# A conformer/SSD block on one core: first pieces' lower halves by adding loads, earlier sums for two units, other banks for the first units, y scaled on ScalarE

## Chip, core and metric

One core of a Trainium2 chip. The metric is the device time of one execution of the program in microseconds (us); less is better. The engines go by these names: PE is TensorE (matmuls), DVE is VectorE, ACT is ScalarE, POOL is GpSimd, and SP issues the loads of weights.

## What is computed

The reference is one block with two branches and a feed forward, all in float32, for 512 tokens of 1024 features:

```python
h = rms_norm(x, mix_pre_g)
proj = h @ w_in
conv_out = conformer_conv_branch(...)     # gated, 31-tap depthwise conv, layer norm, silu, matmul
ssm_out = ssd_branch(...)                 # 4-tap conv, chunked state space scan, then:
#   y = y * silu(z); per group of 256 channels: y * rsqrt(mean(y * y) + eps); y @ out_w
mixed = (g_conv * conv_out + g_ssm * ssm_out) @ w_out
x = x + rms_norm(mixed, mix_post_g)
h = rms_norm(x, ffn_pre_g)
gt, up = jnp.split(h @ w_gate_up, 2, axis=-1)
x = x + rms_norm((silu(gt) * up) @ w_down, ffn_post_g)
```

## The kernel before

Matmuls keep float32 precision by splitting: each operand is cast to a rounded upper half (`hi`), and a lower half (`lo`) is what the cast left over; `mm3` (L165) multiplies hi by hi, hi by lo and lo by hi. So each piece of weights, 128 x 1024, needs a load (`w_raw`, SP, a ring of 5 raw tiles), a cast on ACT and a lower half. In the mixer the lower half has two ways (`w_part`, L131): a subtraction on DVE (L139), or, for every second piece, a negated copy of hi on ACT (L136) and a load from DRAM that adds the raw weights to it, issued by POOL (L137).

The mixer works group by group over 8 groups. `s3` (L588) ends with the norm of y: four squares on ACT (L621), the factor on POOL (`power`), and four multiplications by it on DVE (L624). The transposes of y on PE come in `s4`, one group later.

The output projection (`tm_wo`) runs over four tiles of 128 tokens (t) and eight pieces (k), in the order of `steps`. After a tile's last step `residual(t)` makes the norm, the residual and a diagonal matrix `dg` of the next norm's factors: DVE (L937, L943, L947), ACT (L814) and POOL (L822) take turns. `transposed(t)` multiplies the tile by `dg` (PE, `ptr`, L960), reads the result as `xg`, and makes hi and lo of the moving operands b11, b21, and for odd tiles t1, t2, then in `rest` b22, t3, t4.

The feed forward's gate and up products run over 22 units of 256 columns (u). Each uses a recursion with seven products instead of eight (`product`, 12 matmuls each): `first(u)` (a11 by b11, a12 by b21, into X and Y of a bank), `second(u)` (s2 by t2, s1 by t1, s3 by t3), `third(u)` (s4 by b22, a22 by t4). `second` begins by copying X (ACT, L1075) and adding Y (DVE, L1067), since its s2 product goes on in X. The weights of a unit are two raw pieces. `prep_a` makes hi and lo of the first (a11, a12). `prep_s` makes four sums on DVE (L898 to L903), in the raw tiles, and hi and lo of them: three halves (s2/s4, s1, s3/a22). All go through `halve` (cast on ACT, L877; subtraction on DVE, L878). The tiles for them come in turn from two pools, eight pairs in all (`pair_of_tiles`), so a unit can be prepared when the unit some two and a half before it has been multiplied. Units 0 and 1 have their first pieces prepared at (t, k) = (2, 1). The order within an engine's queue is drawn up by the framework's scheduler from dependencies and program order; `not_before` adds an order without a wait, and `hold` holds those in force.

PSUM has 8 banks; from the output projection on, `bank` (L798) hands them out in turn: `tm_wo` 0 to 7, the transposes of tiles 0 to 2 banks 0 to 5, xy0 and xy1 banks 6 and 7, and so on.

Of the kernel before, what the change touches and what calls it, by code (L numbers as in the profile page):

```python
# [10 lines left out]
F32 = mybir.dt.float32  # L11
# [63 lines left out]
EARLY_U = 4  # L75
DMA_EVERY = 2
DMA_FROM = 8
MOV_AT = 192

TAPS_GLU = 12  # L80
# [29 lines left out]
def block_kernel(ctx: ExitStack, tc: tile.TileContext, x, xT, prm, hp, gp, w, out):  # L110
# [477 lines left out]
    def s3(g):  # L588
        s = st[g]
        hs = slice(HG * g, HG * (g + 1))  # L590
        y = s["y"]
        for n in range(2):
            dve.tensor_tensor(out=y[:, 2 * n : 2 * n + 2], in0=s["yd"][n], in1=y[:, 2 * n : 2 * n + 2], op=ALU.add)
        pa, pb = aux_tile(f"pYa{g}"), aux_tile(f"pYb{g}")
        pY = [None, pa[:, :GW], pa[:, GW:], pb[:, :GW]]
        for c in range(1, NT):
            pe.matmul(
                pY[c], s["C"][:, c * P : (c + 1) * P], s["prev"][:, c - 1].rearrange("p h d -> p (h d)"),
                start=True, stop=True,
            )  # L600
        yo = ssd.tile([P, NT - 1, HG, HD], F32, tag="yo", name=f"yo{g}")
        dve.tensor_tensor(
            out=yo[:, 0:2], in0=pa.rearrange("p (c h d) -> p c h d", c=2, h=HG),
            in1=b3(eacs[:, 1:3, hs], HD), op=ALU.mult,
        )
        dve.tensor_tensor(
            out=yo[:, 2], in0=pb[:, :GW].rearrange("p (h d) -> p h d", h=HG),
            in1=b3(eacs[:, 3, hs], HD), op=ALU.mult,
        )
        dve.tensor_tensor(out=y[:, 1:], in0=y[:, 1:], in1=yo, op=ALU.add)  # L610
        yz = y.rearrange("p c h d -> p c (h d)")
        if "zb" in s:
            for n, zb in enumerate(s["zb"]):
                dve.tensor_tensor(out=yz[:, 2 * n : 2 * n + 2], in0=yz[:, 2 * n : 2 * n + 2], in1=zb, op=ALU.mult)
        else:
            dve.tensor_tensor(out=yz, in0=yz, in1=s["z"], op=ALU.mult)
        ss = ssd.tile([P, NT], F32, tag="ss", bufs=2, name=f"ss{g}")
        rs = ssd.tile([P, NT], F32, tag="rs", bufs=2, name=f"rs{g}")
        for c in range(NT):
            jk = ssd.tile([P, GW], F32, tag="jk", name="jk")  # L620
            act.activation(jk, yz[:, c, :], AF.Square, accum_out=ss[:, c : c + 1])  # L621
        power(rs, ss, 1.0 / GW, RMS_EPS, NT)
        for c in range(NT):
            dve.tensor_scalar(out=yz[:, c, :], in0=yz[:, c, :], scalar1=rs[:, c : c + 1], scalar2=None, op0=ALU.mult)  # L624

    ys = {}

# [167 lines left out]
    dr2 = ctx.enter_context(tc.tile_pool(name="dr2", bufs=1, space=DRAM))  # L795
    x2d = dr2.tile([T, D], F32, name="x2d")

    def bank(name):  # L798
        return in_turn("big", 0, 8, name)

    def tm_tiles(key):
        return [[bank(f"tm_{key}_{t}_{n}") for n in range(2)] for t in range(NT)]
# [69 lines left out]
            w_raw(r)  # L872
        return raws[n]

    def halve(names, u, src, room):
        hi, lo = room
        a_ = act.copy(hi, src)  # L877
        d_ = dve.tensor_tensor(out=lo, in0=src, in1=hi.bitcast(F32), op=ALU.subtract)  # L878
        if hold:
            not_before(a_, hold[0])  # L880
            not_before(d_, hold[1])
        for i, n in enumerate(names):
            c = slice(i * T, (i + 1) * T)
            forms[u, n] = hi[:, c], lo[:, c]

    def prep_a(u, room=None):

        if u < NF and (u, "a11") not in forms:
            halve(("a11", "a12"), u, g_raw(u, 0), room or pair_of_tiles())

    def prep_s(u):

        if u >= NF or (u, "s1") in forms:
            return
        ra, rb_ = g_raw(u, 0), g_raw(u, 1)
        (a11, a12), (a21, a22) = [(r[:, :T], r[:, T:]) for r in (ra, rb_)]
        s1_ = w2.tile([P, T], F32, tag="s1", bufs=2, name=f"s1_{u}")
        sum_ = dve.tensor_tensor(out=s1_, in0=a21, in1=a22, op=ALU.add)  # L898
        if hold:
            not_before(sum_, hold[1])  # L900
        dve.tensor_tensor(out=a21, in0=a11, in1=a21, op=ALU.add)
        dve.tensor_tensor(out=a11, in0=s1_, in1=a11, op=ALU.add)
        dve.tensor_tensor(out=a12, in0=a11, in1=a12, op=ALU.add)  # L903
        halve(("s2", "s4"), u, ra, pair_of_tiles())
        halve(("s1",), u, s1_, [w2.tile([P, T], F32R, tag=tg, bufs=2, name=f"{tg}_{u}") for tg in ("dhi", "dlo")])
        room = pair_of_tiles()

        def last():
            halve(("s3", "a22"), u, rb_, room)

        if u:
            last()
        return last

    def product(ps, u, wn, mn, start):

# [34 lines left out]
    def transposed(t):  # L951
# [2 lines left out]
        xr, dg = xrs[t]  # L954
        xg = []
        for n in range(2):
            pt = bank(f"ptr{t}_{n}").rearrange("p (k q) -> p k q", k=KB)
            for k in range(KB):
                c = slice((KB * n + k) * P, (KB * n + k + 1) * P)
                m = pe.matmul(pt[:, k, :], xr[:, c], dg, start=True, stop=True)  # L960
# [13 lines left out]
        def halved(name, src, sign=1.0):  # L974
# [12 lines left out]
            mark["hi"], mark["lo"] = h_, l_  # L987

        if t % 2 == 0:
            halved("b11", xg[0])  # L990
# [5 lines left out]
        dve.tensor_tensor(out=t1, in0=b11, in1=xg[0], op=ALU.subtract)  # L996
        dve.tensor_tensor(out=t2, in0=t1, in1=xg[1], op=ALU.add)
        halved("t1", t1)
        halved("t2", t2, -1.0)

        def rest():
            halved("b22", xg[1])
# [2 lines left out]
            dve.tensor_tensor(out=t2, in0=t2, in1=b21, op=ALU.subtract)  # L1005
            halved("t4", t2)

        return rest
# [6 lines left out]
    for t, k in steps:  # L1015
# [9 lines left out]
            for u in range(2):  # L1025
                prep_a(u, [m[:, u] for m in first_room])
        if (t, k) == (2, 5):
            others = transposed(1)
        if (t, k) == (3, 5):
            with tc.issue_after(mark["pe"].ins):  # L1030
                transposed(2)

    X, Y, V = {}, {}, {}

    def first(u):

        xy = bank(f"xy{u}")
        X[u], Y[u] = xy[:, :HB], xy[:, HB:]
        product(X[u], u, "a11", "b11", True)
        product(Y[u], u, "a12", "b21", False)  # L1040

    prep_a(2)
    prep_a(3)
    last_s = prep_s(0)
    mark["chain"] = True
    for u in range(3):
        first(u)
    rest = transposed(3)
    pb.close()
    h2e = h2.enter_context(tc.tile_pool(name="h2e", bufs=2))  # L1050
    hold[:] = [mark["hi"], mark["lo"]]
    last_s()
    rest()
    first(3)
    mark["chain"] = False
    prep_s(1)
    hold.clear()
# [5 lines left out]
    sg = {}  # L1063
    c1, c2 = slice(0, HB), slice(HB, T)

    def add(to, ps):
        dve.tensor_tensor(out=to, in0=ps, in1=to, op=ALU.add)  # L1067

    def second(u):
        f, e = u // 2, u % 2  # L1070
        if e == 0:
            dst = sg[f] = [h2e.tile([P, T], F32, tag=f"sg{i}", bufs=2, name=f"sg{f}_{i}") for i in range(2)]
        else:
            dst = [f32[:, 2 * f + i, :] for i in range(2)]
        act.copy(dst[0][:, c1], X[u])  # L1075
        add(dst[0][:, c1], Y[u])
# [173 lines left out]
```

## Time and profile before

| | us |
|---|---|
| median of 3 runs | 1067.81 (1066.97 to 1069.09) |
| profiled execution | 1069.47 |
| its span, first to last instruction | 1067.7 |
| PE busy | 1049.2 (98%) |
| DVE busy | 782.5 (73%) |
| ACT busy | 594.7 (56%) |
| POOL busy | 79.7 (7%) |

A busy share says how long an engine had an instruction in it, not that the instruction ran without a stall. Matmuls overlap, so the distance from one start to the next is what a matmul costs; it is less than its duration. In a timeline a bracket at the end of a line gives the idle time of the engine before the instruction and what ended it. The mixer lasts to about 666 us, the output projection to 714.7, the units of the feed forward to 941.7, the down projection to the end.

### The profile page before, as it was taken

The page shows a single profiled execution, that of the slowest core. Times are in us where ns is not written, and L with a number is a line of the kernel's source. Part 1 is how long each engine was busy: PE and PEld are TensorE (multiplying, and loading weights), DVE is VectorE, ACT ScalarE, POOL GpSimd, SP SyncE. Part 2 cuts the span into 40 slices and gives each one's busy share as a digit, 9 for nine tenths or more (in the row PEclk, how much of TensorE's full clock was granted, in tenths as well). Part 3 has the DMA queues.
Part 4 walks back from the last instruction along what each step waited for, and adds up shares of the span by engine and source line. Part 5 has one row for each costly group of instructions (what it writes and reads, how often), then busy time and mean ns, then how long its engine had stood idle before and what let it go on. Part 6 is the DMA issues. An engine that isn't in the chain of part 4 may idle for free.

```text
span 1067.7 us, 15144 instructions
## 1 busy us (share of the span) xinstructions
PE 1049.2 (98%) x5897; PEld 912.1 (85%) x5897; DVE 782.5 (73%) x1150; ACT 594.7 (56%) x978; POOL 79.7 (7%) x104
## 2 busy tenths in 40 slices
PE   8999999999999999999999999998999999999997
PEld 7988889888888888888888888888999999988886
DVE  7899995977695979497876365569998788643334
ACT  7767749684859375934322672456564554532222
POOL 0002001110111011101100000010000000000000
PEclk9999999999999999999999999999999999999999
DMA  8476653566436553654442232422433243353302
GB/s 294 132 186 209 157 139 89 151 168 165 101 119 159 157 123 116 161 122 111 116 122 82 76 99 79 178 85 93 146 134 118 84 135 100 119 197 99 99 1 79
DMA packets 38088, 136.10 MB, mean 127 GB/s; under 512 B 4480, under 2 KB 4992, under 8 KB 36992
## 3 DMA queue, kind: packets, MB, share of 16 engines
q1 hardware_dynamic: 28368, 97.31, 27.7%
q0 software_dynamic: 6912, 29.36, 13.8%
q10 hardware_dynamic: 2736, 8.46, 2.2%
q8 instruction: 46, 0.75, 0.3%
q14 instruction: 26, 0.21, 0.1%
HBM read 130.85 MB, written 4.26 MB: 127 GB/s over the span
## 4 chain that ended last, share of the span: by engine, by line
PE 79%; DVE 11%; ACT 4%; issue 3%; DMA 1%; POOL 1%; SPq 0%; DVEq 0%; POOLq 0%; ACTq 0%
PE tm_wd L169 4%; PE tm_wd L167 4%; PE tm_wd L168 4%; PE xy L167 3%; PE xy L169 3%; PE xy L168 3%; PE px L169 2%; PE px L168 2%; PE px L167 2%; PE yd L585 2%; PE pz L168 2%; PE pz L169 2%; PE pso L168 2%; PE pz L167 2%; PE pso L169 2%
## 5 line engine op out<-in xcount | busy, mean ns | idle before, releaser
L133 ACT CAST whi<-raw 128x1024 fp32r<-128x1024 f32 (+2 forms) x135 | 137.6, 1029 | 186.6 <-PE pso L168 40.0
L407 DVE SCALAR_TENSOR_TENSOR a<-v,prm_t,a 128x511 f32<-128x511 f32 (+16 forms) x240 | 179.6, 752 | 10.0 <-ACT a L404 7.0
L139 DVE TENSOR_TENSOR wlo<-raw,whi 128x1024 fp32r<-128x1024 f32 (+3 forms) x95 | 112.5, 1187 | 39.5 <-ACT whi L133 39.5
L167 PE MATMUL tm_wd<-whi,fh 128*128 128x512 f32 x160 | 62.2, 389 | 0.0
L168 PE MATMUL tm_wd<-wlo,fh 128*128 128x512 f32 x160 | 62.2, 389 | 0.0
L169 PE MATMUL tm_wd<-whi,fl 128*128 128x512 f32 x160 | 62.2, 389 | 0.0
L137 POOL DMA_DIRECT2D wlo<-in_w x40 | 35.6, 890 | 329.5 <-ACT wlo L136 162.0
L168 PE MATMUL pz<-wlo,hhi 128*128 128x512 f32 (+2 forms) x160 | 56.3, 352 | 0.2
L169 PE MATMUL pz<-whi,hlo 128*128 128x512 f32 (+2 forms) x160 | 55.8, 351 | 0.0
L167 PE MATMUL pz<-whi,hhi 128*128 128x512 f32 (+2 forms) x160 | 55.5, 353 | 0.0
L877 ACT CAST whi_g<-raw 128x1024 fp32r<-128x1024 f32 x40 | 41.1, 1052 | 23.9 <-DVE raw L903 13.0
L878 DVE TENSOR_TENSOR wlo_g<-raw,whi_g 128x1024 fp32r<-128x1024 f32 x40 | 48.0, 1220 | 8.6 <-ACT whi_g L877 8.6
L1120 DVE TENSOR_TENSOR fl<-f,fh 128x512 fp32r<-128x512 f32 x20 | 13.8, 691 | 50.4 <-ACT fh L1119 50.4
L168 PE MATMUL pso<-yl,whi 128*128 128x512 f32 x128 | 49.9, 390 | 0.4 <-DVE yl L639 0.4
L167 PE MATMUL px<-hhi,whi 128*128 128x512 f32 x128 | 50.2, 392 | 0.0
L169 PE MATMUL pso<-yh,wlo 128*128 128x512 f32 x128 | 49.9, 390 | 0.0
L167 PE MATMUL pso<-yh,whi 128*128 128x512 f32 x128 | 49.9, 392 | 0.0
L169 PE MATMUL px<-hhi,wlo 128*128 128x512 f32 x128 | 49.8, 389 | 0.0
L168 PE MATMUL px<-hlo,whi 128*128 128x512 f32 x128 | 49.8, 389 | 0.0
L1119 ACT CAST fh<-f 128x512 fp32r<-128x512 f32 x20 | 12.4, 620 | 60.4 <-PE tm_wd L168 60.4
L390 ACT ACTIVATE L<-L,nacs 128x128 f32<-128x128 f32 x128 | 40.9, 391 | 5.7 <-POOL L L384 5.5
L136 ACT ACTIVATE wlo<-whi 128x1024 fp32r<-128x1024 f32 x40 | 42.3, 1056 | 0.2
(422 smaller groups left out, 3207.8 us busy)
## 6 DMA issues: line engine op xcount, KB each, us to landing
raw<-in_w SPq DMA_DIRECT2D x177, 512.0 KB, 3.6
wlo<-in_w POOLq DMA_DIRECT2D x40, 512.0 KB, 5.6
L<-scr POOLq DMA_DIRECT2D x8, 1024.0 KB, 6.3
xT<-in_xT SPq DMA_DIRECT2D x8, 256.0 KB, 5.4
xr<-in_x ACTq DMA_DIRECT2D x4, 512.0 KB, 4.3
x2d<-xr ACTq DMA_DIRECT2D x4, 512.0 KB, 2.6
x<-x2d ACTq DMA_DIRECT2D x1, 2048.0 KB, 10.3
gpost<-in_gp ACTq DMA_DIRECT2D x2, 512.0 KB, 8.0
```

The lines of the kernel that those rows point to most:

```text
L133: act.copy(hi[:, c], src[:, c])
L136: act.activation(lo[:, c], hi[:, c].bitcast(F32), AF.Copy, scale=-1.0)
L137: pool.dma_start(lo[:, c], w[n][:, c].bitcast(F32R), accum_op=ALU.add)
L139: dve.tensor_tensor(out=lo[:, c], in0=src[:, c], in1=hi[:, c].bitcast(F32), op=ALU.subtract)
L167: mark["pe"] = pe.matmul(ps, lh, rh, start=start, stop=False, skip_group_check=more)
L168: pe.matmul(ps, lh, rl, start=False, stop=False, skip_group_check=more)
L169: mark["pe3"] = pe.matmul(ps, ll, rh, start=False, stop=stop, skip_group_check=more)
L390: act.activation(L[:, h, c, :], L[:, h, c, :], AF.Exp, bias=nacs[:, c, HG * g + h : HG * g + h + 1])
L407: return dve.scalar_tensor_tensor(out=va[j][:, d:], in0=vs[j][:, : T - d], scalar=col("dw_w", j * KC + KC - 1 - d), in1=va[j][:, d:], op0= ...
L585: pe.matmul(yd[c // 2][:, c % 2, h, :], s["L"][:, h, c, :], s["xdt"][:, c, h, :], start=True, stop=True)
L877: a_ = act.copy(hi, src)
L878: d_ = dve.tensor_tensor(out=lo, in0=src, in1=hi.bitcast(F32), op=ALU.subtract)
```

## The change

- `halve` takes an argument `again`. With it, the lower half is not subtracted on DVE: ACT writes the negated hi, and POOL issues a load that adds the raw weights to it, as in the mixer. `prep_a` uses it from unit 2 on (`ADD_FROM`).
- `prep_a(2)` and `prep_a(3)` move from behind the output projection to its steps (3, 1) and (3, 2); the sums of unit 0 (`prep_s(0)`) move to step (3, 4). `prep_s` returns its three halves as a function for units 0 and 1: unit 0's are made before the first products, unit 1's after t1 to t4; unit 1's sums come after `first(0)`.
- `transposed` returns t1 and t2 as a function `sums` of its own, ahead of `rest`. `begin(u)`, the copy of X and the addition of Y, is taken out of `second`; unit 0's comes before `sums` of tile 3. `first(3)` now stands behind unit 1's halves.
- The transposes of tiles 0, 2 and 3 use banks 0 and 1, those of tile 1 banks 2 and 3; xy0 to xy3 use banks 2 to 5; the turn goes on at bank 6.
- In `s3` the four multiplications of y by its factor go from DVE to ACT.

```diff
-            dve.tensor_scalar(out=yz[:, c, :], in0=yz[:, c, :], scalar1=rs[:, c : c + 1], scalar2=None, op0=ALU.mult)
+            act.activation(yz[:, c, :], yz[:, c, :], AF.Copy, scale=rs[:, c : c + 1])
...
-    def bank(name):
-        return in_turn("big", 0, 8, name)
+    def bank(name, n=None):
+        return in_turn("big", 0, 8, name) if n is None else yd_tile(n, name)
...
-    def halve(names, u, src, room):
+    def halve(names, u, src, room, again=None):
+
         hi, lo = room
         a_ = act.copy(hi, src)
-        d_ = dve.tensor_tensor(out=lo, in0=src, in1=hi.bitcast(F32), op=ALU.subtract)
+        if again is not None:
+            d_ = act.activation(lo, hi.bitcast(F32), AF.Copy, scale=-1.0)
+            pool.dma_start(lo, again.bitcast(F32R), accum_op=ALU.add)
+        else:
+            d_ = dve.tensor_tensor(out=lo, in0=src, in1=hi.bitcast(F32), op=ALU.subtract)
...
-            halve(("a11", "a12"), u, g_raw(u, 0), room or pair_of_tiles())
+            again = w[seq[("gu", 2 * u)]] if u >= ADD_FROM else None
+            halve(("a11", "a12"), u, g_raw(u, 0), room or pair_of_tiles(), again)
...
-        halve(("s2", "s4"), u, ra, pair_of_tiles())
-        halve(("s1",), u, s1_, [w2.tile([P, T], F32R, tag=tg, bufs=2, name=f"{tg}_{u}") for tg in ("dhi", "dlo")])
-        room = pair_of_tiles()
-
-        def last():
-            halve(("s3", "a22"), u, rb_, room)
-
-        if u:
-            last()
-        return last
+
+        def halves():
+            halve(("s2", "s4"), u, ra, pair_of_tiles())
+            halve(("s1",), u, s1_, [w2.tile([P, T], F32R, tag=tg, bufs=2, name=f"{tg}_{u}") for tg in ("dhi", "dlo")])
+            halve(("s3", "a22"), u, rb_, pair_of_tiles())
+
+        if u > 1:
+            halves()
+        return halves
...
-            pt = bank(f"ptr{t}_{n}").rearrange("p (k q) -> p k q", k=KB)
+            pt = bank(f"ptr{t}_{n}", 2 * (t == 1) + n).rearrange("p (k q) -> p k q", k=KB)
...
+        if (t, k) in ((3, 1), (3, 2)):
+            prep_a(k + 1)
+        if (t, k) == (3, 4):
+            halves = prep_s(0)
...
-        xy = bank(f"xy{u}")
+        xy = bank(f"xy{u}", 2 + u if u < EARLY_U else None)
...
-    prep_a(2)
-    prep_a(3)
-    last_s = prep_s(0)
+    halves()
     mark["chain"] = True
     for u in range(3):
         first(u)
-    rest = transposed(3)
+        if u == 0:
+            halves = prep_s(1)
+    sums, rest = transposed(3)
     pb.close()
     h2e = h2.enter_context(tc.tile_pool(name="h2e", bufs=2))
-    hold[:] = [mark["hi"], mark["lo"]]
-    last_s()
+    begin(0)
+    sums()
     rest()
+    hold[:] = mark["t3"]
+    halves()
+    hold[:] = mark["t4"]
     first(3)
     mark["chain"] = False
-    prep_s(1)
+    turn["big"] = 1 + EARLY_U
+    prep_s(2)
```

## Rows read from the trace of the kernel before

**Rows 1.** The page's first part: busy us, share of the span, instructions.
```profile
PE 1049.2 (98%) x5897; PEld 912.1 (85%) x5897; DVE 782.5 (73%) x1150; ACT 594.7 (56%) x978; POOL 79.7 (7%) x104
```
**Rows 2.** Stretches: length, busy us (instructions) by engine, granted clock, DMA share, GB/s.
```profile
225.00:680.00 455.00, 452.80 (x2203) 378.45 (x2202) 331.23 (x477) 257.63 (x418) 42.70 (x53) 1.00 0.47 129
714.70:745.50 30.80, 26.51 (x204) 25.42 (x204) 28.05 (x45) 20.00 (x40) 1.72 (x2) 0.94 0.24 75
745.50:768.50 23.00, 23.00 (x204) 23.00 (x204) 22.63 (x35) 12.64 (x21) 0.00 (x0) 1.00 0.45 153
768.50:830.00 61.50, 60.55 (x519) 59.20 (x518) 57.22 (x87) 34.36 (x57) 0.00 (x0) 1.00 0.38 121
830.00:900.00 70.00, 67.95 (x578) 66.79 (x577) 58.27 (x87) 36.68 (x61) 0.00 (x0) 1.00 0.33 106
900.00:941.70 41.70, 41.70 (x370) 41.70 (x369) 26.97 (x44) 19.18 (x34) 0.00 (x0) 1.00 0.32 102
```
**Rows 3.** TensorE's waits, whole span, longest entry: us in total, times, longest.
```profile
PE xy L167 <- DVE sg L1067: 2.8, 4, 1.3
```
**Rows 4.** Timeline of TensorE, 715 to 743: start, us, line, operation [idle before].
```profile
715.74 0.38 PE L167 MATMUL xy<-b11h,a01h 128*128 128x256 f32 x1 [0.88 <-DVE mg L937]
...
724.32 1.95 PE L960 MATMUL ptr<-dg,xr 128*128 128x128 f32 x16
...
729.92 0.35 PE L167 MATMUL xy<-t2h,whi_g 128*128 128x256 f32 x1 [0.79 <-DVE sg L1067]
...
741.97 0.54 PE L169 MATMUL xy<-t2h,clo_g 128*128 128x256 f32 x1 [1.17 <-DVE clo_g L878]
742.30 0.41 PE L167 MATMUL xy<-t2h,chi_g 128*128 128x256 f32 x1
```
**Rows 5.** Timeline of VectorE, 723 to 727.
```profile
723.49 0.29 DVE L947 TENSOR_SCALAR dg<-ident,rs_b 128x128 f32<-128x128 f32 x1 [0.44 <-POOL rs_b L822]
...
725.49 1.22 DVE L878 TENSOR_TENSOR wlo_g<-raw,whi_g 128x1024 fp32r<-128x1024 f32 x1 [0.51 <-ACT whi_g L877]
726.63 0.68 DVE L967 TENSOR_TENSOR xg<-ptr,prm_t 128x512 f32<-128x512 f32 x1
```
**Rows 6.** Timeline of TensorE, two of its later waits.
```profile
845.85 0.39 PE L167 MATMUL xy<-t2h,chi_g 128*128 128x256 f32 x1 [1.31 <-DVE sg L1067]
...
866.69 0.38 PE L167 MATMUL xy<-t2h,whi_g 128*128 128x256 f32 x1 [0.35 <-DVE sg L1067]
```
**Rows 7.** Timeline of VectorE ahead of these two waits.
```profile
844.77 0.69 DVE L898 TENSOR_TENSOR s<-raw 128x512 f32<-128x512 f32 x1 [1.18 <-DMA raw<-in_w]
845.38 0.42 DVE L1067 TENSOR_TENSOR sg<-xy,sg 128x256 f32<-128x256 f32 x1
...
864.75 1.22 DVE L878 TENSOR_TENSOR wlo_g<-raw,whi_g 128x1024 fp32r<-128x1024 f32 x1
...
866.22 0.41 DVE L1067 TENSOR_TENSOR sg<-xy,sg 128x256 f32<-128x256 f32 x1
```
**Rows 8.** Instructions on tile wlo, 100 to 600: duration ns min/median/max, first and last start.
```profile
L136 ACT ACTIVATE wlo<-whi x34: 1040/1051/1086, 105.6 to 539.2; 128x1024 fp32r<-128x1024 f32 x34
```
**Rows 9.** Instructions of line 137, the adding loads of the mixer, and their landing.
```profile
L137 POOL DMA_DIRECT2D wlo<-in_w x40: 857/878/1072, 39.5 to 540.7; - x40
...
DMA to landing us min/median/max: 5.3/5.6/10.7
```
**Rows 10.** Timeline of ScalarE: the cast of the last unit's first piece.
```profile
914.63 1.05 ACT L877 CAST chi_g<-raw 128x1024 fp32r<-128x1024 f32 x1 [0.92 <-PE v L168]
```
**Rows 11.** Timeline of TensorE: the first matmul of the last unit.
```profile
929.46 0.28 PE L167 MATMUL xy<-b11h,chi_g 128*128 128x256 f32 x1
```
**Rows 12.** Timeline of POOL, 700 to 726: the factor of tile 2.
```profile
705.34 0.86 POOL L822 TENSOR_TENSOR rs_a<-pm_a,neg_half 128x1 f32<-128x1 f32 x1 [8.72 <-DVE pm_a L821]
```
**Rows 13.** Instructions of line 624, the scaling of y, and its engine's idle time.
```profile
L624 DVE TENSOR_SCALAR y<-y,rs x32: 345/348/354, 178.9 to 532.5; 128x256 f32<-128x256 f32 x32
...
  POOL rs L176: 27.9, 8
```
**Rows 14.** Instructions of line 621, the squares of y on ScalarE.
```profile
L621 ACT ACTIVATE jk<-y x32: 399/413/431, 170.2 to 529.5; 128x256 f32<-128x256 f32 x32
```

More of the change, by code (lines that the diff above doesn't have):

```diff
@@ L77 @@
 DMA_FROM = 8
+ADD_FROM = 2
 MOV_AT = 192
@@ L873, in g_raw @@
         return raws[n]
-    def halve(names, u, src, room):
+    def halve(names, u, src, room, again=None):
         hi, lo = room
         a_ = act.copy(hi, src)
-        d_ = dve.tensor_tensor(out=lo, in0=src, in1=hi.bitcast(F32), op=ALU.subtract)
+        if again is not None:
[3 more added lines that the diff above has]
+            d_ = dve.tensor_tensor(out=lo, in0=src, in1=hi.bitcast(F32), op=ALU.subtract)
         if hold:
             not_before(a_, hold[0])
-            not_before(d_, hold[1])
+            not_before(d_, hold[again is None])
         for i, n in enumerate(names):
@@ L986, in halved @@
                 not_before(l_, mark["lo"])
-            mark["hi"], mark["lo"] = h_, l_
+            mark["hi"], mark["lo"] = mark[name] = h_, l_
         if t % 2 == 0:
@@ L995, in transposed, with sums @@
         t1, t2 = [pmp.tile([P, KB, P], F32, tag=f"t{i}", bufs=1, name=f"t{i}_{t}") for i in (1, 2)]
[L996 to L999, printed above, removed]
+        def sums():
+            dve.tensor_tensor(out=t1, in0=b11, in1=xg[0], op=ALU.subtract)
+            dve.tensor_tensor(out=t2, in0=t1, in1=xg[1], op=ALU.add)
+            halved("t1", t1)
+            halved("t2", t2, -1.0)
         def rest():
@@ L1006, in rest @@
             halved("t4", t2)
-        return rest
+        return sums, rest
     for k in range(2, NK):
@@ L1027, in block_kernel @@
         if (t, k) == (2, 5):
-            others = transposed(1)
+            sums, others = transposed(1)
+            sums()
[3 more added lines that the diff above has]
+            halves = prep_s(0)
         if (t, k) == (3, 5):
@@ L1031, in block_kernel, with add, begin @@
                 transposed(2)
+    sg = {}
+    c1, c2 = slice(0, HB), slice(HB, T)
+    def add(to, ps):
+        dve.tensor_tensor(out=to, in0=ps, in1=to, op=ALU.add)
+    D_ = {}
+    def begin(u):
+        f, e = u // 2, u % 2
+        if e == 0:
+            sg[f] = D_[u] = [h2e.tile([P, T], F32, tag=f"sg{i}", bufs=2, name=f"sg{f}_{i}") for i in range(2)]
+        else:
+            D_[u] = [f32[:, 2 * f + i, :] for i in range(2)]
+        act.copy(D_[u][0][:, c1], X[u])
+        add(D_[u][0][:, c1], Y[u])
     X, Y, V = {}, {}, {}
     def first(u):
-        xy = bank(f"xy{u}")
+        xy = bank(f"xy{u}", 2 + u if u < EARLY_U else None)
         X[u], Y[u] = xy[:, :HB], xy[:, HB:]
@@ L1047, in block_kernel @@
         first(u)
-    rest = transposed(3)
+        if u == 0:
+            halves = prep_s(1)
+    sums, rest = transposed(3)
     pb.close()
     h2e = h2.enter_context(tc.tile_pool(name="h2e", bufs=2))
-    hold[:] = [mark["hi"], mark["lo"]]
-    last_s()
+    begin(0)
+    sums()
     rest()
+    hold[:] = mark["t3"]
+    halves()
+    hold[:] = mark["t4"]
     first(3)
     mark["chain"] = False
-    prep_s(1)
+    turn["big"] = 1 + EARLY_U
+    prep_s(2)
     hold.clear()
@@ L1062, in block_kernel @@
     f32 = fp.tile([P, NF, T], F32, name="f32")
[L1063 to L1067, printed above, removed]
     def second(u):
[L1070 to L1076, printed above, removed]
+        if u not in D_:
+            begin(u)
+        dst = D_[u]
         product(X[u], u, "s2", "t2", False)
```

## The prediction, made before the change was run

> **What bounds the kernel now.** I read the page's first part, then a table of stretches, then TensorE's waits, then the timelines of TensorE and VectorE where it waits. The profiled execution took 1069.47 us, 1067.7 of them span; the median of the three runs shown is 1067.81. The sum is made on the profiled execution, and its result is carried over to the median, 1.66 us lower.
>
> TensorE is busy for 98% of the span [rows 1], so a change pays only where TensorE stands still, or runs at the lower clock. The table of stretches finds the places, if each is compared with what its matmuls need [rows 2]. From 900 on the feed forward runs without a gap: 370 matmuls in 41.70 us, 0.1127 us each. At that pace the 204 matmuls from 714.7 to 745.5 need 22.99 us and take 30.80: **7.8 us lost**. From 745.5 to 768.5 nothing is lost. From 768.5 to 830, 519 matmuls need 58.5 of 61.5: 3.0 lost. From 830 to 900, 578 need 65.1 of 70: 4.9 lost. Together 15.7 us, and that is the most the feed-forward edits can give. In the mixer (225 to 680) TensorE is idle for 2.2 us of 455, so there is next to nothing to win there. From 900 to the down projection at 941.7 TensorE has no gap in which a gain could be swallowed: what the units give back reaches the end.
>
> What is late? In the first stretch VectorE is busy for 28.05 of 30.80 us, in the next for 22.63 of 23: it works off a backlog. The longest entry of TensorE's waits is an addition of VectorE, L1067, for which a unit's second series waits [rows 3]. One by one [rows 4]: at 715.74 the first product waits 0.88 us for `mg` of L937, which reads the bank that xy0 is given; at 729.92 the s2 product of unit 0 waits 0.79 for the addition L1067; at 741.97 unit 1's s2 product waits 1.17 for a lower half. The other gaps of the stretch are smaller. Behind this run of short gaps the granted clock falls: the matmul at 742.30 takes 0.41 us [rows 4], and the mean of the stretch is 0.94 where the other stretches have 1.00 [rows 2]. A mean of 0.94 over 30.8 us is 3.7 us at the lower of the clock's two levels (1.2 and 2.4 GHz), and half of that, about 1.8 of the 7.8 us, is lost by it. VectorE's timeline shows why t2 is late: the transposes of tile 3 start at 724.32 [rows 4], but their `xg` is read only at 726.63, since a 1.22 us lower half of unit 0 (725.49) is ahead of it [rows 5].
>
> In the later stretches the gaps are of two kinds. At 866.69 the s2 product waits for the addition of 866.22 [rows 6], which stood behind the 1.22 us lower half of 864.75 [rows 7]; that half is the one whose cast waits until late for its tiles, the first piece of the next unit. At 845.85 the product waits 1.31 for an addition behind the sum of 844.77, which itself waited 1.18 for a load of raw weights [rows 6, 7].
>
> **The change part by part.** (1) *Lower halves by adding loads.* For units 2 to 21, 20 subtractions leave VectorE, 1.22 us each in the rows, 1.15 from start to start: 23 us in all, 1.15 per unit of 84 x 0.1127 = 9.5 us. ScalarE gets 20 negated copies. The trace has that very pair in the mixer: the copy takes 1.05 us [rows 8], the issue on POOL 0.88, the landing 5.6 (at most 10.7) [rows 9]. ScalarE is busy for 83.7 of the 154.5 us from 745.5 to 900 [rows 2]; about 16 units there add some 16, 65%. POOL has nothing else to do from 745 on. What hides the longer way to a lower half is the lead of the cast: the last unit's first piece is cast at 914.63 [rows 10] and multiplied at 929.46 [rows 11], 14.8 us later. Cast, copy, issue and landing need 1.05 + 1.05 + 0.88 + 5.6 = 8.6 us, with the longest row of each 13.9. So the cost is nothing by the middle and nothing, just, by the worst. The copy may stand on ScalarE ahead of the copy of X for L1067: at worst 1.05 us, less than the 1.15 that the addition loses ahead of it on VectorE.
>
> (2) *Sums, halves and the addition of unit 0 earlier.* Unit 0's four sums (each 0.69 us in the rows, 0.61 from start to start [rows 7]) move into tile 3's projection, where TensorE runs on whole; its three halves come before the first products; unit 1's sums follow them; `begin(0)` is put ahead of t1 and t2, and unit 0's second half no longer sits between them. Work on VectorE is the same, but the 1.22 us ahead of `xg` and the halves of unit 0 among t1 to t4 are gone. So `xg` can be read some 2.2 us sooner, 1.1 because TensorE transposes sooner without the wait at 715.74, 1.1 because the half ahead of it (725.49 to 726.63) is gone, while the s2 product comes 1.1 sooner. Of its wait of 0.79 nothing need be left; but behind the addition stand t2's own halves, so I keep 0.5, between 0 and 0.79. Since unit 0's raw tiles are free sooner, unit 1's second piece is loaded sooner too, and units 1 and 2 should be ready before TensorE gets there: the waits at 741.97 and around it go, and with them the fall of the clock. What is next late: the diagonal matrix dg of tile 3. It was ready at 723.78 [rows 5], and TensorE would now be there at about 723.2: 0.5 us, unless it also comes sooner, which it may, since two lower halves that stood ahead of its inputs on VectorE are replaced by others.
>
> (3) *Banks.* xy0 to xy3 take banks 2 to 5, free long before; the 0.88 us at 715.74, with the restart 1.0, go. Next late are the halves of b11 and b21 for tile 2, which VectorE makes in these same microseconds: 0 to 0.9 us, I take 0.3.
>
> (4) *New load on the queues in tile 3's projection.* Casts, copies and issues for units 2 and 3 (4 x 1.05 on ScalarE, 2 x 0.88 on POOL) fall among the steps of tile 2's norm. POOL makes `rs_a` there at 705.34 [rows 12]; an issue ahead of it that waits for its copy would hold up the norm and then tile 2's transposes, for which TensorE waits. Bounds: 0, if they come in idle time, to 1.05 + 0.88 = 1.9 us. I take 0.5, nearer to the lower end, since POOL had stood idle for 8.72 us before that row and the casts' tiles come free about when tile 3's projection begins.
>
> (5) *y scaled on ScalarE.* 32 operations of 0.35 us leave VectorE [rows 13], 32 of about 0.41 (the same shape at L621 [rows 14]) come to ScalarE. The wait for the factor, 27.9 us in 8 places [rows 13], moves from VectorE to ScalarE's queue, where the casts of weights stand behind it. By TensorE's 2.2 us of idle time this can give at most 2.2; it can cost as much again if a cast comes late. I take 0.
>
> ScalarE is the slower engine here by the rows, 0.41 against 0.35. The Trainium skill (page "ScalarE: Activation LUTs", section "Rules for kernel authors") says to multiply on VectorE, not ScalarE; the trace agrees on the single operation, and by that rule the edit would cost 32 x 0.06 = 2 us (my estimate) if ScalarE were the bound, which it is not.
>
> The sum: the first stretch keeps 0.5 (t2) + 0.5 (dg) + 0.3 (b11) + 0.3 of restarts of its 7.8 us: gain 6.2. New queue load: -0.5. Of the later 7.9 us about half is behind first pieces' lower halves or the backlog and goes, and half is behind raw loads and stays: gain 4. In all 9.7, so 1069.47 - 9.7 = 1059.8 for the profiled execution, **1058.1** for the median. All of the 15.7 would be 1052.1.
>
> **The rivals.** *Only the first stretch pays.* VectorE now catches up at about 745 instead of 800, and then meets the raw loads earlier; a sum at the head of its queue that waits 1.2 us holds the additions of 16 units, not 7. The later loss then stays at about 8 us, and the time is 1067.8 - 5.7 = 1062.1. For it: the wait at 844.77 belongs to the time without backlog. Against it: from 768.5 to 830 VectorE still worked for 57 of 61.5 us, and only 3.0 were lost; and the halves that made it wait late are gone.
>
> *The relay.* In the transition the chain tile 3's norm, dg, transposes, t1, t2 is what the products wait for, and the earlier work only moves the wait there; with the 1.9 us of (4) in full and as much at dg, the gain falls to 6.2 - 3.8 = 2.4, with nothing later: 1065.4.
>
> *Slower: lower halves that land late.* Place: the third matmul of a unit's first product. It decides when the time from cast to landing exceeds the lead. If tiles come free one unit later than now, the lead is 14.8 - 9.5 = 5.3 us against 8.6, 3.3 us lost in each of 18 units: 59 us less the gain, about 1116. A lateness of only 0.8 us in each would already cost 14 and end at 1072. Against it: in the mixer 40 such loads are issued [rows 9], and TensorE is idle there for 2.2 us in all [rows 2]. The Trainium skill (page "SBUF — State Buffer", section "Who interferes with whom") says that a two-input VectorE operation contends with GpSimd's reads and that descriptor generation can be starved by VectorE; the issue of 0.86 to 1.07 us [rows 9] beside a VectorE that is busy for 331 us of 455 [rows 2] shows no such block, and one 1.22 us operation waited out would still leave the lead whole.
>
> *Nothing moves*: the order of the queues, drawn up ahead, makes as many new waits as it removes: 1067.
>
> **How the numbers follow.** Forecast 1058.1 (1053 to 1061): 0.50. Only the first stretch, 1062.1 (1060 to 1064): 0.20. The relay, 1065.4 (1063.5 to 1067): 0.13. Nothing, 1067 to 1069: 0.08. Slower by late landings, 1072 and more: 0.09. The range 1053 to 1067 holds the first three. A measurement of this kernel can tell about 0.2%, 2.1 us: faster means below 1065.7. That is the first two and 0.08 of the relay: 0.78. Same: the rest of the relay and most of "nothing": 0.12. Slower: 0.10.
>
> **What would show it.** TensorE's wait for `mg` at the first product is gone; the granted clock stays at 1.00 through the transition; the stretch from the first product to the tenth microsecond of unit 2 has no wait above 0.6 us; VectorE's busy share after 750 is near 80% instead of 98%; POOL has 20 issues from 704 on, and no wait of TensorE names a lower half. The prediction is wrong if TensorE waits at a unit's third matmul, if tile 2's transposes come late, or if the additions L1067 still stand behind waits for raw loads in most units.

## The result, and the profile after

The changed kernel takes **1071.89 us**, median of 8 runs (1070.16 to 1076.09), against 1067.78 of 8 runs of the kernel before beside them: ratio 1.0041, 95% interval 1.0024 to 1.0057. It is slower by 4.1 us, where 9.7 us of gain were forecast, and outside the range of 1053 to 1067. The profiled execution of it took 1070.62 us, 1068.8 of them span.

The page's first part and its POOL row, and from the sixth part two rows of loads (out<-in, engine, count, size, median us from issue to landing):
```profile
PE 1050.1 (98%) x5897; PEld 913.7 (85%) x5897; DVE 753.1 (70%) x1098; ACT 620.6 (58%) x1026; POOL 99.3 (9%) x124
...
wlo_g<-in_w POOLq DMA_DIRECT2D x13, 512.0 KB, 5.8
clo_g<-in_w POOLq DMA_DIRECT2D x7, 512.0 KB, 5.6
```
Against [rows 1] VectorE has lost 29 us of work and ScalarE gained 26, as the change says, and POOL has its 20 issues. The work moved; the time did not follow. The stretches of the kernel after, in the columns of [rows 2], the first product being at 712.63 instead of 715.74:
```profile
711.60:742.40 30.80, 28.09 (x226) 26.64 (x225) 28.27 (x46) 20.31 (x42) 2.48 (x2) 1.00 0.42 122
742.40:765.40 23.00, 20.39 (x177) 20.07 (x176) 20.52 (x33) 15.45 (x22) 2.63 (x3) 1.00 0.75 203
765.40:827.00 61.60, 60.42 (x517) 59.10 (x516) 47.09 (x74) 38.74 (x60) 5.22 (x6) 1.00 0.64 162
827.00:897.00 70.00, 67.42 (x562) 66.28 (x562) 49.43 (x79) 40.78 (x65) 5.25 (x7) 0.98 0.59 157
897.00:942.90 45.90, 45.50 (x398) 45.10 (x397) 26.19 (x43) 23.43 (x40) 2.58 (x3) 1.00 0.47 127
```
By the prediction's own reckoning, 0.1127 us for each matmul, the stretches lose 5.3, 3.1, 3.3, 6.7 and 1.0 us, 19.4 together, where the kernel before lost 7.8, 0, 3.0, 4.9 and 0, 15.7. So the transition gains 2.5 us of the 6.2 forecast, about half of it because its clock stays at 1.00 (e4 below does that without the change), and the later part, from which 4 us of gain were expected, loses 6.2 us more. Read the DMA column too: 203, 162, 157 and 127 GB/s where [rows 2] have 153, 121, 106 and 102. VectorE is no longer full (47.09 of 61.6 us, where it was busy for 57.22 of 61.5). From the first product to the first matmul of the down projection pass 230.2 us, before 226.0; 4.2 us more, about the 4.1 by which the medians differ.

TensorE's waits from 711 to 950 (us in total, times, longest):
```profile
PE xy L170 <- DMA wlo_g<-in_w: 2.6, 1, 2.6
PE xy L168 <- DVE sg L1050: 1.9, 1, 1.9
PE v L168 <- ACT dhi L879: 1.5, 1, 1.5
PE xy L168 <- ACT sg L1104: 1.4, 3, 0.7
PE xy L168 <- DVE f L1050: 1.4, 3, 0.6
PE ptr L966 <- issue: 0.4, 1, 0.4
```
The wait for `mg` at the first product is gone, and the first matmul of xy0 at 712.63 follows the last of the output projection at 712.40. Other waits stand in its place. The longest in the timelines of TensorE, POOL and ScalarE, in this order:
```profile
753.42 0.28 PE L168 MATMUL xy<-b11h,whi_g 128*128 128x256 f32 x1
753.53 0.28 PE L169 MATMUL xy<-b11l,whi_g 128*128 128x256 f32 x1
756.41 0.39 PE L170 MATMUL xy<-b11h,wlo_g 128*128 128x256 f32 x1 [2.61 <-DMA wlo_g<-in_w]
```
```profile
749.02 0.89 POOL L882 DMA_DIRECT2D wlo_g<-in_w  x1 [27.43 <-DVE sg L1050]
```
```profile
746.34 1.05 ACT L879 CAST whi_g<-raw 128x1024 fp32r<-128x1024 f32 x1
...
747.55 1.07 ACT L881 ACTIVATE wlo_g<-whi_g 128x1024 fp32r<-128x1024 f32 x1
```
This is unit 4: its cast comes at 746.34, and its first product at 753.42, so the lead is 7.1 us, while cast, copy, issue and a landing of 7.4 us take until 756.4. The second is at 845.36, behind VectorE's rows of the same microseconds; at the same place before, TensorE waited 1.31 [rows 6, 7]:
```profile
845.36 0.38 PE L168 MATMUL xy<-t2h,chi_g 128*128 128x256 f32 x1 [1.85 <-DVE sg L1050]
```
```profile
842.62 0.69 DVE L905 TENSOR_TENSOR s<-raw 128x512 f32<-128x512 f32 x1 [2.77 <-DMA raw<-in_w]
843.35 0.69 DVE L908 TENSOR_TENSOR raw<-raw,raw 128x512 f32<-128x512 f32 x1
843.96 0.68 DVE L909 TENSOR_TENSOR raw<-s,raw 128x512 f32<-128x512 f32 x1
844.56 0.42 DVE L1050 TENSOR_TENSOR f<-v,f 128x256 f32<-128x256 f32 x1
844.89 0.41 DVE L1050 TENSOR_TENSOR sg<-xy,sg 128x256 f32<-128x256 f32 x1
```
The sum of 842.62 has stood at the head of VectorE's queue for 2.77 us, waiting for a raw load (1.18 before), and the addition of 844.89, for which TensorE waits, is four places behind it. Behind this wait the clock falls, which costs some 1.4 us more: the stretch that follows has 19 matmuls in 3.50 us, at 0.1127 each 2.1 us of work:
```profile
846.70:850.20 3.50, 3.50 (x19) 3.50 (x19) 2.33 (x3) 2.82 (x5) 0.00 (x0) 0.53 0.39 76
```
VectorE's waits for raw loads, after and before:
```profile
DVE s L905 <- DMA raw<-in_w: 15.9, 11, 2.8
```
```profile
DVE s L898 <- DMA raw<-in_w: 6.0, 5, 1.3
```
Not all waits for additions (`sg` and `f`) are new: in this profile TensorE spends 3.3 us on them, in the profile before 4.3. What the adding loads cost is therefore read from runs that differ in them alone.

### The profile page after: what moved, and what is told of

It is laid out like the page before. It is cut to its first block, busy times and chain, and to the rows that moved or that the text cites. A ratio compares the mean times of both kernels' runs of the same rounds, so it can differ in the third digit from the quotient of the medians.

```text
span 1068.8 us, 15192 instructions
## 1 busy us (share of the span) xinstructions
PE 1050.1 (98%) x5897; PEld 913.7 (85%) x5897; DVE 753.1 (70%) x1098; ACT 620.6 (58%) x1026; POOL 99.3 (9%) x124
## 3 DMA queue, kind: packets, MB, share of 16 engines
q0 software_dynamic: 9792, 39.85, 19.4%
## 4 chain that ended last, share of the span: by engine, by line
PE 79%; DVE 9%; DMA 5%; ACT 5%; issue 1%; POOL 0%; SPq 0%; DVEq 0%; POOLq 0%; ACTq 0%
DMA raw<-in_w 4%; PE tm_wd L170 4%; PE tm_wd L169 4%; PE tm_wd L168 4%; PE pso L169 3%; PE pso L170 2%; PE pso L168 2%; PE xy L168 2%; PE px L168 2%; PE px L170 2%; PE px L169 2%; PE yd L586 2%; PE xy L170 2%; PE xy L169 2%; PE pz L170 2%; PE pz L169 2%
## 5 line engine op out<-in xcount | busy, mean ns | idle before, releaser
L879 ACT CAST whi_g<-raw 128x1024 fp32r<-128x1024 f32 x40 | 41.4, 1053 | 37.4 <-PE xy L169 18.8
L884 DVE TENSOR_TENSOR wlo_g<-raw,whi_g 128x1024 fp32r<-128x1024 f32 x27 | 32.5, 1223 | 14.7 <-ACT whi_g L879 14.6
```

## The experiments

**The theories.** A: the adding loads cost, by their traffic, which makes the raw loads of the next units late. B: the new order of the transition costs. C: the scaling of y on ScalarE costs. Within A three ways are to be told apart: the lower halves land late; VectorE and ScalarE have a worse order; or slow raw loads reach TensorE through a sum that stands ahead of an addition.

The measured ratios to the kernel before, with what the traces show from 711 to 950: TensorE's waits summed over all entries, VectorE's waits for raw loads (us, times, longest), and the median landing of a raw load from 743 to 930.

| kernel | median us | ratio [95%] | TensorE waits | raw waits | landing |
|---|---|---|---|---|---|
| before | 1067.8 | 1 | 7.1 | 6.0, 5, 1.3 | 3.7 |
| after | 1071.89 | 1.0041 [1.0024, 1.0057] | 9.2 | 15.9, 11, 2.8 | 4.4 |
| e1 no adding loads | 1068.42 | 0.9995 [0.9982, 1.0009] | 6.0 | 6.1, 6, 1.2 | 3.6 |
| e2 y on VectorE | 1072.82 | 1.0042 [1.0026, 1.0059] | 8.6 | 15.1, 11, 2.9 | 4.3 |
| e3 adding loads alone | 1079.10 | 1.0095 [1.0077, 1.0113] | 12.7 | 16.3, 9, 3.4 | 4.3 |
| e4 y on ScalarE alone | 1069.62 | 1.0007 [0.9995, 1.0019] | 7.1 | 5.9, 5, 1.4 | 3.6 |
| f1 no traffic | 1066.95 | 0.9981 [0.9971, 0.9992] | 4.2 | 11.7, 11, 1.6 | 3.6 |
| f2 traffic beside | 1074.06 | 1.0047 [1.0030, 1.0064] | 9.3 | 10.7, 8, 2.6 | 4.2 |
| f5 adding from unit 6 | 1072.22 | 1.0034 [1.0023, 1.0044] | 7.4 | 14.0, 9, 2.7 | 4.4 |
| f6 e1, s1 first | 1066.67 | 0.9981 [0.9971, 0.9991] | 3.5 | 6.2, 6, 1.3 | 3.6 |
| f3 after, ordered | 1066.24 | 0.9982 [0.9969, 0.9995] | 5.0 | 2.6, 2, 2.0 | 4.0 |
| g7 f6, ordered | 1064.00 | 0.9954 [0.9937, 0.9970] | 3.0 | 0.8, 1, 0.8 | 3.6 |
| g8 g7 with adding loads | 1065.18 | 0.9973 [0.9961, 0.9985] | 4.0 | 0.9, 2, 0.5 | 4.1 |
| h1 before, ordered | 1065.87 | 0.9984 [0.9974, 0.9994] | 5.0 | 0.7, 1, 0.7 | 3.7 |

The ratio grows with TensorE's waits, though f5 (7.4 us, 1.0034, where the kernel before has 7.1 us) shows that one profile of each kernel doesn't rank them exactly. Up to the output projection, profiles of kernels with the same code there differ by up to 3.2 us (it starts at 663.7 to 666.9 us), so traces are compared from there on, and times only by the ratios.

**e1: the change without its adding loads** (the subtractions stay on VectorE).
```diff
-ADD_FROM = 2
+ADD_FROM = NF
```


> The changed kernel, with all first pieces' lower halves subtracted on VectorE again; early sums, banks and y on ScalarE stay. Theory A (the adding loads cost: unit 4's lower half lands 2.6 us late, and VectorE waits 15.9 us instead of 6.0 for raw loads, with the additions behind): the rest of the change is worth what was forecast for the transition, so about 1062 to 1065, below the kernel before, and VectorE's waits for raw loads go back to about 6 us. Rival B (the new order of the transition costs): stays at 1070 to 1073. Rival C (y on ScalarE costs in the mixer): stays at 1070 to 1073 too.

Measured: 0.9995. A holds: the adding loads cost the changed kernel 0.46%, 4.9 us by the two ratios. But the 1062 to 1065 us that came with A are missed: the rest of the change, which should have gained over 6 us in the transition, brings nothing that can be measured, and B falls with it, since the new order alone costs nothing either.

**e2: the change with y scaled on VectorE again**, and **e4: the kernel before with y scaled on ScalarE**, the one edit of that line each way.

> The changed kernel with y scaled on VectorE again, all else as changed. Theory A and rival B: no difference from the changed kernel, 1071 to 1073. Rival C: back to about 1067 to 1068, and the mixer before the output projection shorter by about 4 us in the timed runs.

> The kernel before with y scaled on ScalarE and nothing else. Theory A and rival B: 1067 to 1069, no difference. Rival C: 1071 to 1073.

Measured: 1.0042 beside the changed kernel's 1.0041, and 1.0007 with 1 in its interval. C falls; the edit is worth nothing, either way.

The trace of e4 shows something else. From the output projection on its code is that of the kernel before, and so are TensorE's waits to the end of the transition (1.2, 0.9, 0.8, 0.7 us and two of some 0.3), but its clock stays up. Its first product is at 714.14, so this is the stretch of 714.70 to 745.50 before:
```profile
713.10:743.90 30.80, 26.58 (x215) 25.11 (x215) 28.77 (x46) 21.04 (x41) 1.43 (x2) 1.00 0.22 77
```
That is 215 matmuls, where the kernel before has 204 at 0.94 [rows 2] and the changed kernel 226. So whether the clock falls behind such waits differs from one execution to the next; of the 22 matmuls that the changed kernel is ahead in the transition, 11 are the clock's and 11, some 1.2 us, the change's.

**e3: the kernel before with adding loads alone**, from unit 4 on (`halve` and `prep_a` as in the change, `ADD_FROM = 4`).

> The kernel before with adding loads for the first pieces of units 4 to 21 and nothing else of the change. Theory A: slower than before, 1069 to 1073, with VectorE's waits for raw loads at 12 us or more and landings of raw weights at 4.0 us or more in the units. Rival B: the forecast's gain in the later units shows undisturbed, 1063 to 1066. Rival C: the same as B.

Measured: 1.0095, more than twice the loss of the whole change and well above the 1069 to 1073 us expected. TensorE's longest waits:
```profile
PE xy L170 <- DMA wlo_g<-in_w: 3.5, 1, 3.5
PE xy L168 <- DVE sg L1073: 3.3, 2, 2.5
PE xy L168 <- DVE f L1073: 2.5, 3, 1.4
```
They are the two kinds of the kernel after, the late lower half and the late addition, and larger. That speaks against B once more: with the transition of before the adding loads cost more, not less. Why twice as much, no run shows.

**f1: the changed kernel without the loads themselves**, all other work and its order kept.
```diff
             d_ = act.activation(lo, hi.bitcast(F32), AF.Copy, scale=-1.0)
-            pool.dma_start(lo, again.bitcast(F32R), accum_op=ALU.add)
```


> The changed kernel with the 20 adding loads left out and everything else kept: ScalarE still makes the negated copy, VectorE still makes no subtraction for units 2 to 21, so the lower half of these first pieces holds only the negated upper half (this part of the computation is left out). It tells what the loads themselves cost (their traffic and their landing) from what the other load and order on VectorE and ScalarE cost. Theory 'traffic and landing': the waits of VectorE for raw loads fall from 15.9 us back to about 6, the raw loads land in 3.6 us again instead of 4.3 to 4.4, TensorE's wait of 2.6 us for unit 4's lower half goes, the stretch from the first product to the first down-projection matmul falls from 230.2 to 225 us or less, and the time is 1066 to 1068.5 us. Rival 'order of the engines': the sums still stand ahead of the additions and reach the raw loads early, the waits stay above 12 us and the time at 1070.5 to 1073 us.

Measured: 0.9981; 0.60% below the changed kernel with the same instructions on VectorE (1098) and ScalarE (1026), in the same order in both traces. The loads are the cost, not the copies or the order that they brought. Two expectations missed: from the first product to the down projection pass 225.7 us, not 225 or less, and the waits for raw loads stay 11, and 11.7 us. What shrinks is each of them. The place of 842.62 in f1's timeline of VectorE, and TensorE behind it:
```profile
841.83 0.69 DVE L904 TENSOR_TENSOR s<-raw 128x512 f32<-128x512 f32 x1 [1.14 <-DMA raw<-in_w]
```
```profile
844.57 0.39 PE L168 MATMUL xy<-t2h,chi_g 128*128 128x256 f32 x1 [0.22 <-DVE sg L1049]
```
The sum waits 1.14 instead of 2.77, and TensorE 0.22 instead of 1.85: the difference is the same 1.63 us, handed on whole.

**f2: e1, with adding loads whose result nobody reads** (for units 4 to 20, into rows of `f32` that are not used until the last unit).
```diff
+            if u in SPARE:
+                for i, n in enumerate(("a11", "a12")):
+                    act.activation(to[:, i, :], forms[u, n][0].bitcast(F32), AF.Copy, scale=-1.0)
+                pool.dma_start(to, w[seq[("gu", 2 * u)]].rearrange("p (i t) -> p i t", i=2), accum_op=ALU.add)
```


> The changed kernel without adding loads for its halves (the subtractions stay on VectorE, as in the run without adding loads, 1068.4 us), but with 17 adding loads of the same 512 KB, for units 4 to 20, into a place that nobody reads, after a negated copy on ScalarE. No product waits for them, so it prices their traffic and the copies without their landing. Theory 'the traffic delays the raw loads': the raw loads land in about 4.3 us instead of 3.6, VectorE's waits for raw loads are over 12 us, and the time is 1070.5 us or more. Rival 'only the late landing costs' (TensorE waiting for unit 4's lower half, and the clock after it): 1068 to 1069 us, with waits for raw loads near 6 us.

Measured: 1.0047, as slow as the changed kernel, though no product waits for these loads and VectorE keeps its subtractions. The raw waits are fewer than expected (10.7 us), but long, up to 2.6, and the largest of TensorE's waits is for an addition:
```profile
PE xy L169 <- DVE sg L1056: 5.0, 4, 2.3
```
So a late landing is not what costs most: the traffic does. The copies on ScalarE come with it here; in f1, where they take the place of the subtractions, they cost nothing, and beside the subtractions they were not tried alone.

**f5: adding loads from unit 6 on** (`ADD_FROM = 6`).

> The changed kernel with adding loads from unit 6 on instead of unit 2: four of the 20 are gone, those around the transition, unit 4's late one among them. Theory 'one late landing at the start': the 2.6 us wait at unit 4 and the lower clock after it go, and the time is 1068 to 1069 us, level with no adding loads at all. Theory 'the traffic delays the raw loads in every unit': 16 of 20 stay, VectorE's waits for raw loads stay above 11 us, and the time is 1070 to 1071.5 us. If unit 6's own first load now lands late in the same way, a wait of 2 to 3 us shows at unit 6's first product and the time is as in the changed kernel, 1071 to 1073 us.

Measured: 1.0034. Unit 4's late half is gone, no other comes in its place, and most of the loss stays, so the theory of one late landing falls. What that landing costs, these runs don't resolve: the interval of f5 overlaps that of the changed kernel.

**f3: the changed kernel, with the sum of unit u held behind the opening addition of unit u-3 on VectorE.**
```diff
         sum_ = dve.tensor_tensor(out=s1_, in0=a21, in1=a22, op=ALU.add)
+        if u - 3 in began:
+            not_before(sum_, began[u - 3])
```
with `began[u]` set to the addition in `begin`.

> The changed kernel with its 20 adding loads and one more constraint on the order: on VectorE the sum of unit u may not stand ahead of the addition that opens unit u-3 (L1050), so a sum that waits for its raw load no longer holds the addition that TensorE needs. The loads' traffic is as before. Theory 'slow raw loads reach TensorE through VectorE's order': the wait of 1.85 us at 845.36 and its like go, the waits for raw loads stay above 10 us, and the time falls from 1071.9 to 1068.5 to 1070 us (unit 4's late lower half, 2.6 us, stays). Rival 'the raw loads themselves set the pace' (the sum, moved back, makes the halves late): waits for halves take the place of those for the addition, and the time stays at 1071 to 1073 us.

Measured: 0.9982, 0.59% below the changed kernel, with all 20 adding loads in place and raw loads that still land in 4.0 us. VectorE's rows at the place of 842.62, now without a wait on a load:
```profile
842.35 0.69 DVE L911 TENSOR_TENSOR raw<-s,raw 128x512 f32<-128x512 f32 x1 [1.93 <-ACT whi_g L879]
842.96 0.42 DVE L1052 TENSOR_TENSOR f<-v,f 128x256 f32<-128x256 f32 x1
843.29 0.41 DVE L1052 TENSOR_TENSOR sg<-xy,sg 128x256 f32<-128x256 f32 x1
...
845.15 0.68 DVE L905 TENSOR_TENSOR s<-raw 128x512 f32<-128x512 f32 x1
```
The addition is ready at 843.29 and the sum comes after it, when its load has long landed. The stretch from 827 to 897 then holds 601 matmuls in 70 us, after 562:
```profile
827.18:897.18 70.00, 69.99 (x601) 69.34 (x600) 52.12 (x82) 45.12 (x72) 6.08 (x7) 1.00 0.68 163
```
I had expected raw waits above 10 us and a time of 1068.5 to 1070; they fall to 2.6, and the time is lower. So the path is traffic, slower raw load, waiting sum, late addition, TensorE: the same order gives 0.59% where the adding loads run and 0.16% on the kernel before (h1), a difference clear of noise. It is not the whole of f3's gain: TensorE's waits for additions fall from 3.3 to 1.2 us, but its wait for unit 4's lower half also falls, from 2.6 to 0.9, with a landing of some 5.9 us instead of 7.4.

**f6: e1, with unit 1's s1 piece halved ahead of its s2 and s4 piece.**
```diff
+            def one():
+                halve(("s1",), u, s1_, [w2.tile([P, T], F32R, tag=tg, bufs=2, name=f"{tg}_{u}") for tg in ("dhi", "dlo")])
+
+            if u == 1:
+                one()
             halve(("s2", "s4"), u, ra, pair_of_tiles())
-            halve(("s1",), u, s1_, [w2.tile([P, T], F32R, tag=tg, bufs=2, name=f"{tg}_{u}") for tg in ("dhi", "dlo")])
+            if u != 1:
+                one()
```


> The changed kernel without adding loads (1068.4 us), and with one thing turned round in the transition: unit 1's s1 piece is cut into halves ahead of its s2 and s4 piece. In the run without adding loads TensorE waited 1.51 us at 734.5 us for that s1 half, which stood on ScalarE behind the wider cast. Theory 'relay' (what the early sums and the banks gain is taken back by the next operand in line): this wait goes and 0.5 to 1.5 us come through, 1066.9 to 1067.9 us, unless the s2 half takes its place, which then shows as a wait at the product with s2. Rival 'the transition has no gain to give': 1068 to 1069 us, with the waits between 711 and 743 us adding up to as much as before.

Measured: 0.9981. ScalarE and TensorE in e1 at this place:
```profile
732.38 1.04 ACT L879 CAST chi_g<-raw 128x1024 fp32r<-128x1024 f32 x1
733.33 0.61 ACT L983 CAST t4h<-t 128x512 fp32r<-128x512 f32 x1
733.85 0.61 ACT L879 CAST dhi<-s 128x512 fp32r<-128x512 f32 x1
734.37 1.04 ACT L879 CAST chi_g<-raw 128x1024 fp32r<-128x1024 f32 x1
735.32 0.36 ACT L1104 COPY sg<-xy 128x256 f32<-128x256 f32 x1
```
```profile
734.52 0.38 PE L168 MATMUL v<-t1h,dhi 128*128 128x256 f32 x1 [1.51 <-ACT dhi L879]
...
735.73 0.39 PE L168 MATMUL xy<-t3h,chi_g 128*128 128x256 f32 x1 [0.71 <-ACT sg L1104]
...
736.29 0.41 PE L168 MATMUL xy<-t3h,chi_g 128*128 128x256 f32 x1
```
In e1 TensorE waits 1.51 us for `dhi`, which stands behind a wide cast, then 0.71 for a copy behind the second; and after these gaps the matmuls take 0.41 us instead of 0.28. In f6 both waits shrink (0.5 for `dlo`, 0.3 for the copy) and the clock stays up, as the same stretch shows in e1 and in f6:
```profile
714.52:745.32 30.80, 27.69 (x210) 26.34 (x209) 26.53 (x43) 20.13 (x44) 2.08 (x2) 0.94 0.26 87
```
```profile
713.23:744.03 30.80, 28.99 (x235) 27.45 (x233) 28.15 (x46) 20.45 (x44) 2.07 (x2) 1.00 0.28 94
```
So the order of two casts held part of the transition's gain. How large a part is less sure: part of the 25 matmuls between these rows is the clock, which differs between executions, and the intervals of e1 and f6 overlap. Against the kernel before f6 gains 0.19%, 2.0 us of the 6.2 forecast.

**g7 and g8: f6 with the order of f3, without and with the adding loads**; **h1: the kernel before with that order alone.**

> The changed kernel without adding loads, with unit 1's s1 halves first (together 1066.7 us) and with the addition ahead of the sum. In the kernel with the first two the waits for the addition behind a sum are 1.9 us, 2 times. Theory 'VectorE's order': these go and the time is 1064.5 to 1066 us; rival 'the waits only move to the halves': 1066.5 to 1067.5 us.

> As the kernel without adding loads, with unit 1's s1 halves first and the addition ahead of the sum, but with the 20 adding loads of the changed kernel. The difference between the two is the price of the adding loads once no sum stands in front of an addition. Theory 'VectorE's order is the path by which the traffic costs': under 2.5 us above it, unit 4's late lower half alone, 1066.5 to 1068 us. Rival 'the traffic costs whatever the order': 4 us or more above it, as between the changed kernel and the one without adding loads (3.5 us).

> The kernel before with nothing of the change, and only the constraint that the sum of unit u may not stand ahead of the addition that opens unit u-3 on VectorE. In the kernel before, TensorE waits 2.8 us, 4 times, for that addition (1.5 us at 845.85 and 0.8 us at 866.69 among them). Theory 'VectorE's order costs by itself': these waits go and the time falls by 1.5 to 3 us, to 1065 to 1066.5 us. Rival 'the order matters only with the adding loads' traffic': 1067.5 to 1068.5 us, the waits having moved to the halves.

Measured: g7 0.9954, 1064.00 us and the fastest of all; g8 0.9973; h1 0.9984. The order pays without any adding load (h1: the raw waits fall from 6.0 to 0.7 us), pays again on top of f6, and with it the adding loads' price is 2.0 us by the ratios of g8 and g7, whose intervals overlap, where it was 4.9; unit 1's s1 halves differ too, and the fall by itself is not clear of noise. In g8 TensorE's largest wait is unit 4's lower half again, 2.2 us, and no wait for an addition is in its list. The expected 1066.5 to 1068 us for g8 and 1064.5 to 1066 for g7 were both a little too high.

## Why the prediction was wrong

**Adding loads (part 1), costed at nothing: the step that failed.** The sum counted what VectorE, ScalarE and POOL do and when the halves land. It left out that each first piece is read from memory a second time, beside the raw loads of later units: 512 KB more per unit, and a raw load takes 4.4 us instead of 3.7. f2 prices that traffic, with its copies, at 0.52% over e1, 5.6 us, though nobody waits for its result. The bytes alone understate it. The two queues of the kernel after from 743 to 930, SP's plain loads first (packets, MB, time of the packets as a share of the 16 DMA engines'):
```profile
q1 hardware_dynamic: 5668, 20.60, 31.5%
q0 software_dynamic: 2592, 9.44, 30.5%
```
Under a third of the bytes takes half of the packets' time: a packet of an adding load lasts about twice as long as a plain one of the same size. The plain packets last no longer than in e1, where 5941 take 35.2%. Whether the bytes or the long packets make the raw loads late was not tried; plain loads in place of the adding ones would tell. The Trainium skill (page "DMA: Bandwidth & Descriptors", section "Issuing engines are not separate DMA queues") says that transfers started by different engines run on the same 16 DMA engines and interleave there; the trace agrees, 3.6 us for a raw load in e1 and 4.2 in f2, where all that is added to the DMA engines' work comes from POOL's queue.

**The later gain of 4 us.** I split the later loss into halves that lower halves and raw loads cause, and let the second half "stay". It could not stay: less work lets VectorE reach the sums sooner (f1: 11 waits for raw loads instead of 5), and more traffic makes each wait longer (after: up to 2.8 us, f1 up to 1.6). The rival "only the first stretch pays" had this mechanism, a sum at the head of the queue, but kept each wait at 1.2 us. What a wait costs hangs on where the addition stands, too: at the same place a sum that waits 1.14 us leaves TensorE 0.22 in f1, one that waits 1.18 leaves it 1.31 in the kernel before [rows 6, 7], and 2.77 leave it 1.85 in the kernel after. That these waits cost without any adding load is what h1 shows.

**The lead of 14.8 us** was read off the last unit [rows 10, 11] and taken for all. Unit 4, cast in the transition, has 7.1. The rival "slower" named the right place, a unit's third matmul, but there it happens once, for 2.6 us, not in every unit; that its time for 0.8 us in each, 1072, lies beside the measured 1071.9 is luck. (Its first sum comes to 1058.1 + 59, which is 1117 and not 1116.)

**Banks (part 3): right.** The 0.88 us [rows 4] and the restart are gone. **New load in tile 3's projection (part 4): 0.5 was too much in the kernel after**, where TensorE has no wait at tile 2's transposes; the 0.41 at tile 3's is the dg term of part 2, for which 0.5 was right:
```profile
708.56 1.95 PE L966 MATMUL ptr<-dg,xr 128*128 128x128 f32 x16
...
722.02 2.02 PE L966 MATMUL ptr<-dg,xr 128*128 128x128 f32 x16 [0.41 <-issue]
```
**It was too little without the adding loads**: in e1 VectorE makes the lower halves of units 2 and 3 just ahead of tile 2's dg, and TensorE waits 0.70 us for the transposes behind it, and 0.77 for those of tile 3:
```profile
708.25 2.35 DVE L884 TENSOR_TENSOR wlo_g<-raw,whi_g 128x1024 fp32r<-128x1024 f32 x2
...
711.45 0.29 DVE L953 TENSOR_SCALAR dg<-ident,rs_b 128x128 f32<-128x128 f32 x1 [0.72 <-POOL rs_b L823]
```
**Sums and halves earlier (part 2): the mechanism was right, the size not.** t2 comes in time, and the wait of 0.79 is gone; the 1.8 us set down for the clock were no sure gain, since e4 has them without the change; and I looked for the next late operand at dg and on VectorE alone. It was on ScalarE, 1.5 us for unit 1's s1 half, and 0.7 for the copy behind it: the rival "the relay", at another place than I gave it. **y (part 5): right**, nothing (e2, e4).

Of the signs that the prediction named, the wait for `mg` is gone, the clock stays at 1.00 through the transition (which e4 shows to be no proof), VectorE is busy for 76% of the stretch from 765.4, and POOL has its 20 issues. Others failed: the transition has waits of 1.52 and 0.71 us, and TensorE waits for a lower half. Two stand that it had set down as refuting it: TensorE waits at a third matmul (756.41), and sums with additions behind them wait for raw loads 11 times.

## What to carry to other kernels

A transfer that takes work off an engine is not free because its own landing is hidden: count its bytes, and the time that its packets take, against the loads that run beside it, and ask who waits for those. An in-order engine hands a late load on to everything queued behind it, so before taking work off it, look whether an instruction that waits for a load stands ahead of one that the bottleneck waits for; putting the urgent one first gave 1.7 us on the kernel before with one constraint, and 6.3 us on the changed one. A lead has to be read at its shortest place, not at the last unit.

## What the runs showed of the hardware

The adding loads, 512 KB each, land in 5.5 to 5.6 us in the middle, but the three issued between 735 and 765, around the stretch with a DMA share of 0.75, took 7.3 to 7.9. Plain loads of 512 KB on the other queue slow from 3.6 to 4.2 or 4.4 us when one adding load per unit of some 10 us is put beside them, although the DMA engines are busy for 0.59 to 0.64 of those stretches only.

TensorE's clock fell to its lower level (granted 0.94 over the stretch) in e1, behind waits of 0.77, 1.51 and 0.71 us, and stayed at 1.00 in the kernel after behind 0.41, 1.52 and 0.71, and in f6 behind smaller ones. In the kernel before it fell, and in e4 it stayed, behind the same waits. A short stall can thus cost more than its length, in some executions and not in others: the mean granted clock of the 23 runs of the kernel before beside e1 goes from 0.995 to 0.999, so one profile does not show whether a kernel has such a fall.
